# Combined blocks of the output weights made early and kept in DRAM; pair sums of y on VectorE

## The chip, the cores and the metric
The kernel runs on one core of one Trainium2 chip. The metric is device time in microseconds (us) of one execution. The kernel before took 882.3 us, the median of three runs (879.62 to 882.65).

Engines are named as in the profile: PE is TensorE (matmuls), PEld its weight loads, DVE is VectorE, ACT is ScalarE, POOL is GpSimd, and SP is the queue from which all DMAs here are issued.

## The reference
One layer on x, 2048 positions of 1024 channels, float32:

```python
h = rmsnorm(x, g_pre) * (1 + scale) + shift          # scale, shift, gate from c
gu, gv, gg, rq, rk, rv, rg = split(h @ w_in)         # seven parts of 512 columns
y_gmlp = gu * (tril(w_s) LN(gv) + b) * silu(gg)      # chunks of 128 positions, 4 groups
y_ret = GroupNorm(retention(rope(rq), rope(rk), rv)) * silu(rg)   # 4 heads, chunkwise
y = concat(y_gmlp, y_ret) @ w_out                    # 2048 x 1024 times 1024 x 1024
x = x + gate * rmsnorm(y, g_post)
```

The change touches the last product, y @ w_out, only.

## The kernel before, in words
**Precision.** Each float32 operand of a large product is split into a high part of reduced precision (`wh`, `yh`, `hh`, made by a copy on ACT) and a rest (`wl`, `yl`, `hl`, made by a subtraction on DVE). A product of two blocks is then three matmuls (`mm3`, L256 to L258), each with 512 columns.

**Halves and units.** The 2048 positions are worked in two halves. In each half four passes over h make retention's v, q and k and gMLP's v; then come six units of 28 ticks, which make the gates and u. A unit multiplies two by two blocks of weights with two by two blocks of h by a Strassen-Winograd scheme: seven products instead of eight, in the order of PRODUCTS, with sums of blocks on both sides (A11, S2, A12, S3, S1, A22, S4 on the one, B11, T2, B21, T3, T1, T4, B22 on the other), gathered in the PSUM banks X, Y and Z. A bank is reopened for a later product: the third product goes on in X, the fourth and sixth in Y, the seventh in Z. What is read from a bank in between (`s1` by a copy on ACT, `u2` and `u3` by adds on DVE, written `u` in the profile) must be read before the bank's next product starts. In the units POOL makes the sums of weight blocks (L241).

**The out stage.** y @ w_out uses the same scheme. Its A side are pairs of chunks: position block ch and position block ch + 4 of a half, eight pairs in all. The y blocks are spilled to DRAM (`yspill`, L614) and read back a pair at a time (`ya`, L624). `pair_sums` makes S1 to S4 of a pair (`ys`, L634): on DVE for the first group, which interleaves two pairs, and on POOL for the six single pairs behind it. Each of a pair's seven operands is then split (`yh` on ACT L643, `yl` on DVE L644), six ticks ahead of its product. `out_tail` reads the banks: adds (L694), squares with row sums on ACT (L691), the root on POOL (L698, L699), gains (L705), the result (L708) and its store (L710).

**Output weights.** 28 blocks (seven products times four of the inner dimension) of 128x512 are needed, and stay in SBUF once they are split. `pump` takes the next one in a fixed order: `wdma` loads it and the next two or three (L190), and `wsplit` splits it (L198, L201). B11, B21 and B22 are blocks of `wout`. The T blocks are combined by `osplit`: at T2 the blocks B12, B11 and B22 are loaded, and two DVE operations make T3 and T2 (L215, L216); T3 is kept in SBUF until its turn; T1 is made by one DVE operation at its own turn (L220), and T4 by one more from B21, loaded a second time (L224). The splits of a combined block start a tick later. B11 is pumped at the end of the fifth unit and the start of the sixth, T2, B21 and T3 in the sixth unit, T1, T4 and B22 in the first group, one block each second tick.

**What sets the order.** The instructions of PE, DVE, ACT and POOL stand in the order in which the program gives them, and each engine works through its own in order. The program goes by ticks: `slots.tick()` before each group of three matmuls runs what is due, and `slots.at(n, f)` makes f due n ticks later. A tick is three matmuls. SP's order is chosen by the compiler from what is ready; SP too works in order, so a DMA that waits holds those behind it.

**SBUF.** Most tiles of 128x512 come from one pool of 80 slots (`slot`).

Of the kernel before, what the change touches and what calls it, by code (L numbers as in the profile page):

```python
# [11 lines left out]
F32 = mybir.dt.float32  # L12
# [4 lines left out]
ALU = mybir.AluOpType  # L17
# [4 lines left out]
P = 128  # L22
# [23 lines left out]
PRODUCTS = (("B11", "A11"), ("T2", "S2"), ("B21", "A12"), ("T3", "S3"), ("T1", "S1"), ("T4", "A22"),  # L46
            ("B22", "S4"))
# [53 lines left out]
def tile_hybrid_layer(ctx: ExitStack, tc, x, xt, wm, wg, win, wun, wout, wst, cols, rows, pos, cst,  # L101
                      invf, out):
    nc = tc.nc
    V, S, G, T, SP = nc.vector, nc.scalar, nc.gpsimd, nc.tensor, nc.sync
# [4 lines left out]
    ps_m = ctx.enter_context(tc.tile_pool(name="ps_m", bufs=4, space=PSUM))  # L109
    ps_s = ctx.enter_context(tc.tile_pool(name="ps_s", bufs=4, space=PSUM))  # L110

    slots = Slots()
    ctx.enter_context(tc.manual_schedule(engines=ORDERED))

# [27 lines left out]
    def slot(name, shape=(512,), dtype=F32, pool=None):  # L142
        return (pool or big).tile([P, *shape], dtype, name=name, tag="s")
# [9 lines left out]
    def closed(n=1):  # L153
        for _ in range(n):
# [3 lines left out]
    raw, blocks = {}, {}  # L158
# [1 line left out]
    PER_HALF = IN_BLOCKS + len(UNITS) * len(PRODUCTS)  # L160
    OUT_BLOCKS = 2 * PER_HALF
    ALL_BLOCKS = OUT_BLOCKS + 4 * len(PRODUCTS)
    OUT_RAW = {"B11": ("B11",), "T2": ("B12", "B11", "B22"), "B21": ("B21",), "T3": (),
               "T1": (), "T4": ("B21",), "B22": ("B22",)}

    def place(i):
        if i >= OUT_BLOCKS:
            return "out", 0, i - OUT_BLOCKS
        half, i = divmod(i, PER_HALF)
        if i < IN_BLOCKS:  # L170
            return "in", half, i
        return "unit", half, i - IN_BLOCKS

    def wdma(i):
        kind, half, n = place(i)
        if kind == "unit":
            un = n // len(PRODUCTS)
            if (half, un) not in raw:
                raw[half, un] = {}
                for k, key in enumerate(("B11", "B12", "B22", "B21")):  # L180
                    t = raw[half, un][key] = slot("ur")
                    SP.dma_start(t, wun[un, (0, 1, 3, 2)[k]])
            return
        if i in raw or i in blocks:
            return
        if kind == "out":
            raw[i] = {}
            for key in OUT_RAW[PRODUCTS[n // 4][0]]:
                t = raw[i][key] = slot("or")
                SP.dma_start(t, wout[int(key[2]) - 1, 4 * int(key[1]) - 4 + n % 4])  # L190
            return
        raw[i] = slot("wr")
        SP.dma_start(raw[i], win[n // KB, n % KB])

    def split(i, r, eng, gap):
        hi, lo = slot("wh", dtype=F32R), slot("wl", dtype=F32R)
        blocks[i] = (hi, lo)
        S.copy(hi, r)  # L198

        def rest():  # L200
            eng.tensor_tensor(lo, r, hi.bitcast(F32), ALU.subtract)  # L201

        if gap:
            slots.at(gap - 1, rest)
        else:
            rest()

    kept = {}

    def osplit(i, n, eng, gap):  # L210
        r, (p, kb) = raw.pop(i), divmod(n, 4)
        what = PRODUCTS[p][0]
        if what == "T2":
            t3, t2, t1 = kept["T3", kb], kept["T2", kb], kept["T1", kb] = r["B12"], r["B11"], r["B22"]
            V.tensor_tensor(t3, t1, t3, ALU.subtract)  # L215
            V.tensor_tensor(t2, t3, t2, ALU.add)  # L216
            slots.at(1, lambda: split(i, t2, eng, gap))
        elif what == "T1":
            t = kept.pop((what, kb))
            V.tensor_tensor(t, t, kept["T2", kb], ALU.subtract)  # L220
            slots.at(1, lambda: split(i, t, eng, gap))
        elif what == "T4":
            t = r["B21"]
            V.tensor_tensor(t, t, kept.pop(("T2", kb)), ALU.subtract)  # L224
            slots.at(1, lambda: split(i, t, eng, gap))
        else:
            split(i, kept.pop((what, kb)) if what == "T3" else r[what], eng, gap)

    def wsplit(i, eng=V, gap=1):
        wdma(i)  # L230
        kind, half, n = place(i)
        if kind == "out":
            return osplit(i, n, eng, gap)
        if kind == "in":
            return split(i, raw.pop(i), eng, gap)
        r = raw[half, n // len(PRODUCTS)]
        what = PRODUCTS[n % len(PRODUCTS)][0]

        def combine(name, a, b):
            r[name] = slot("ut")  # L240
            G.tensor_tensor(r[name], r[a], r[b], ALU.subtract)  # L241

        if what == "T2":
            combine("T1", "B12", "B11")
            combine("T2", "B22", "T1")
        elif what == "T3":
            combine("T3", "B22", "B12")
        elif what == "T4":
            combine("T4", "B21", "T2")
        if what in ("T2", "T3", "T4"):  # L250
            slots.at(3, lambda: split(i, r[what], eng, gap))
        else:
            split(i, r[what], eng, gap)
# [9 lines left out]
    def pump(eng=V, gap=1, ahead=3):  # L263
        if done[0] < len(worder):
            wsplit(worder[done[0]], eng, gap)
            done[0] += 1
        for i in worder[done[0]:done[0] + ahead]:
            wdma(i)
# [334 lines left out]
            slots.at(delay + t, fn)  # L603


    ydram = ctx.enter_context(tc.tile_pool(name="ydram", bufs=1, space=bass.MemoryType.DRAM))
    yd = {}

    def yspill(half, part, cols):
# [7 lines left out]
    def pair_loads(half, ch):  # L617
        a = {}

        def load():  # L620
            for m in range(2):
                for part in range(2):
                    t = a[f"A{m + 1}{part + 1}"] = slot("ya", (4, P), pool=areas[0])
                    SP.dma_start(t, yd[half, part, m][:, ch, :, :])  # L624

        return a, load

    def pair_sums(a, ops, size, j):

        def op(out, x, y, how):  # L630
            def run():
                if out not in a:
                    a[out] = slot("ys", (4, P))
                (V if size > 1 else G).tensor_tensor(a[out], a[x], a[y], how)  # L634
                if out == "S3":
                    a.pop("A21")
            return run

        def part(key):
            def run():  # L640
                hi, lo = ops[key] = slot("yh", (4, P), F32R), slot("yl", (4, P), F32R)
                src = a[key]
                S.copy(hi, src)  # L643
                slots.at(0, lambda: V.tensor_tensor(lo, src, hi.bitcast(F32), ALU.subtract))  # L644
            return run

        def need(n):
            return 4 * (size * n + j)

        n = [need(i) for i in range(len(PRODUCTS))]  # L650
        return ((n[0] - 8, op("S1", "A21", "A22", ALU.add)), (n[0] - 6, part("A11")),
                (n[1] - 9, op("S2", "S1", "A11", ALU.subtract)), (n[1] - 6, part("S2")),
                (n[3] - 12, op("S3", "A11", "A21", ALU.subtract)), (n[2] - 6, part("A12")),
                (n[3] - 6, part("S3")), (n[6] - 17, op("S4", "A12", "S2", ALU.subtract)),
                (n[4] - 6, part("S1")), (n[5] - 6, part("A22")), (n[6] - 6, part("S4")))
# [456 lines left out]
    def prepare(group, at):  # L1112

        for j, (_, _, ops, a, load) in enumerate(group):
            slots.at(at - 20 + 4 * j, load)
            for t, fn in pair_sums(a, ops, len(group), j):
                slots.at(at + t, fn)
# [26 lines left out]
    for half in range(2):  # L1144
# [56 lines left out]
        for un in range(len(UNITS)):  # L1201
            if un == 0:
                for n, fn in enumerate(late):
                    slots.at(1 + 3 * (n // 2) + n % 2, fn)
            if un == 2:
                slots.at(5, partial(yspill, half, 0, range(HEADS)))
            if un == 4:
                slots.at(6, partial(yspill, half, 1, (0, 1)))
            if half == 0 and un in BUILD:
                for t, what, *args in BUILD[un]:  # L1210
                    slots.at(t, partial({"diag": diag1, "row": row1, "x": fetch1, "h": build1}[what],
                                        *args))
            if half == 1 and un == len(UNITS) - 1:
                groups = []
                for size in GROUPS_OUT:
                    groups.append([])
                    for i in range(size):
                        n = sum(GROUPS_OUT[:len(groups) - 1]) + i
                        groups[-1].append((*divmod(n, QUAD), {}, *pair_loads(*divmod(n, QUAD))))
                prepare(groups[0], len(PRODUCTS) * 4)  # L1220
            unit(half, un, up)
# [78 lines left out]
```

## Time and profile before

| | |
|---|---|
| three runs | 882.3, 882.65, 879.62 us |
| profiled execution, own time | 881.76 us |
| its span in the profile | 880.0 us |
| PE busy | 845.7 us (96%), 4074 instructions |
| DVE busy | 673.3 us (77%), 1275 instructions |
| ACT busy | 313.0 us (36%) |
| POOL busy | 358.1 us (41%) |
| granted TensorE clock, mean | 0.995 |
| DMA | 100.59 MB, mean 114 GB/s |

The profiled execution's own time is 1.76 us more than the span, which runs from the first to the last instruction in the profile. A busy share is a mean over stages with different limits. In the profile's rows `out<-in` gives the tiles that an instruction writes and reads, a name in brackets behind "idle before" is what ended a wait, and the line number is that of the kernel printed above. The second half's units run from 591 to 709 us, the out stage's first group from 709 to 752 us, and the six single pairs from there to 869 us.

### The profile page before, as it was taken

The page shows a single profiled execution, that of the slowest core. Times are in us where ns is not written, and L with a number is a line of the kernel's source. Part 1 is how long each engine was busy: PE and PEld are TensorE (multiplying, and loading weights), DVE is VectorE, ACT ScalarE, POOL GpSimd, SP SyncE. Part 2 cuts the span into 40 slices and gives each one's busy share as a digit, 9 for nine tenths or more (in the row PEclk, how much of TensorE's full clock was granted, in tenths as well). Part 3 has the DMA queues.
Part 4 walks back from the last instruction along what each step waited for, and adds up shares of the span by engine and source line. Part 5 has one row for each costly group of instructions (what it writes and reads, how often), then busy time and mean ns, then how long its engine had stood idle before and what let it go on. Part 6 is the DMA issues. An engine that isn't in the chain of part 4 may idle for free.

```text
span 880.0 us, 11841 instructions
## 1 busy us (share of the span) xinstructions
PE 845.7 (96%) x4074; PEld 696.3 (79%) x4074; DVE 673.3 (77%) x1275; ACT 313.0 (36%) x611; POOL 358.1 (41%) x403
## 2 busy tenths in 40 slices
PE   1999999999999999999999999999999999899996
PEld 0778888888888888888888888888888767688884
DVE  3989885665996768997786665897448898978885
ACT  4674223232363334431111221345343444333331
POOL 2031264345756236300443234675566000644551
PEclk9999999999999999999999999999999999999998
DMA  8971331310013424654222100011424854565422
GB/s 321 329 266 37 96 105 64 96 37 1 1 60 96 133 72 155 198 173 155 60 72 74 49 1 1 1 49 37 121 83 151 280 187 149 184 180 163 144 106 86
DMA packets 61884, 100.59 MB, mean 114 GB/s; under 512 B 5888, under 2 KB 22400, under 8 KB 61824
## 3 DMA queue, kind: packets, MB, share of 16 engines
q1 hardware_dynamic: 61824, 99.83, 34.6%
q8 instruction: 32, 0.52, 0.2%
q14 instruction: 28, 0.23, 0.1%
HBM read 83.03 MB, written 16.78 MB: 113 GB/s over the span
## 4 chain that ended last, share of the span: by engine, by line
PE 84%; DVE 6%; issue 3%; DMA 3%; ACT 2%; POOL 1%; SPq 0%; DVEq 0%; POOLq 0%; ACTq 0%
PE pqk L258 6%; PE pqk L256 6%; PE pqk L257 6%; PE pY L258 4%; PE pY L256 4%; PE pY L257 3%; PE pv L256 3%; PE pv L258 3%; PE pv L257 3%; PE prv L257 3%; PE prv L256 2%; PE pX L256 2%; PE prv L258 2%; PE pX L258 2%; PE pX L257 2%
## 5 line engine op out<-in xcount | busy, mean ns | idle before, releaser
L256 PE MATMUL pqk<-wh,hh 128*128 128x512 f32 x240 | 102.5, 427 | 0.0
L524 POOL TENSOR_TENSOR rA<-rA,rB 128x512 f32<-128x512 f32 x32 | 42.9, 1340 | 133.4 <-DVE rB L516 96.5
L258 PE MATMUL pqk<-wh,hl 128*128 128x512 f32 x240 | 94.7, 394 | 0.0
L257 PE MATMUL pqk<-wl,hh 128*128 128x512 f32 x240 | 93.8, 391 | 0.0
L538 ACT COPY qkT<-tp 128x512 f32<-128x512 f32 x32 | 18.8, 588 | 160.1 <-PE tp L529 160.1
L698 POOL TENSOR_SCALAR zrs<-zss 128x1 f32<-128x1 f32 x16 | 18.2, 1140 | 128.7 <-ACT jz L691 128.0
L201 DVE TENSOR_TENSOR wl<-wr,wh 128x512 fp32r<-128x512 f32 x62 | 63.0, 1030 | 0.2
L258 PEld LDWEIGHTS pqk<-wh,hl 128*128 128x128 f32 x240 | 45.0, 188 | 10.6
L256 PE MATMUL pv<-wh,hh 128*128 128x512 f32 x128 | 52.1, 407 | 0.0
L257 PEld LDWEIGHTS pqk<-wl,hh 128*128 128x128 f32 x240 | 45.5, 189 | 6.7 <-issue 0.2
L256 PEld LDWEIGHTS pqk<-wh,hh 128*128 128x128 f32 x240 | 45.4, 189 | 6.5 <-issue 0.2
L258 PE MATMUL pv<-wh,hl 128*128 128x512 f32 x128 | 50.1, 391 | 0.0
L257 PE MATMUL pv<-wl,hh 128*128 128x512 f32 x128 | 50.0, 390 | 0.0
L514 DVE TENSOR_TENSOR rA<-pqk,cos_t 128x512 f32<-128x512 f32 x28 | 19.3, 688 | 32.0 <-PE pqk L258 32.0
L201 DVE TENSOR_TENSOR wl<-ut,wh 128x512 fp32r<-128x512 f32 x48 | 42.9, 913 | 0.5 <-ACT wh L198 0.3
L582 DVE TENSOR_SCALAR yq<-o,gmv,grs 128x128 f32<-128x128 f32 x64 | 23.3, 405 | 23.9 <-POOL grs L575 23.9
L241 POOL TENSOR_TENSOR ut<-ur,ut 128x512 f32<-128x512 f32 x24 | 35.8, 1492 | 13.6 <-DVE yT L790 7.2
L461 ACT ACTIVATE vh<-pv,nbv,rsv 128x128 f32<-128x128 f32 x64 | 24.2, 457 | 47.4 <-POOL nbv L456 47.4
L256 PE MATMUL zY<-wh,yh 128*128 128x512 f32 x96 | 38.2, 398 | 2.2 <-DVE u L694 2.2
L198 ACT CAST wh<-ut 128x512 fp32r<-128x512 f32 x48 | 28.7, 621 | 31.7 <-POOL ut L241 31.7
L258 PE MATMUL zY<-wh,yl 128*128 128x512 f32 x96 | 38.3, 399 | 1.2 <-DVE yl L644 1.2
L790 POOL TENSOR_TENSOR yT<-yT,c 128x512 f32<-128x512 f32 x15 | 24.5, 1638 | 35.9 <-DVE c L810 25.8
(258 smaller groups left out, 2571.1 us busy)
## 6 DMA issues: line engine op xcount, KB each, us to landing
wr<-in_win SPq DMA_DIRECT2D x64, 256.0 KB, 3.9
ur<-in_wun SPq DMA_DIRECT2D x48, 256.0 KB, 3.5
slab<-in_wm SPq DMA_DIRECT2D x16, 512.0 KB, 6.2
ya<-yd SPq DMA_DIRECT2D x32, 256.0 KB, 3.8
xr<-in_x SPq DMA_DIRECT2D x16, 512.0 KB, 5.2
out<-xr SPq DMA_DIRECT2D x32, 256.0 KB, 2.8
or<-in_wout SPq DMA_DIRECT2D x28, 256.0 KB, 3.1
xt<-in_xt SPq DMA_DIRECT2D x24, 256.0 KB, 4.2
```

Of the source, the lines that this page charges most:

```text
L198: S.copy(hi, r)
L201: eng.tensor_tensor(lo, r, hi.bitcast(F32), ALU.subtract)
L241: G.tensor_tensor(r[name], r[a], r[b], ALU.subtract)
L256: T.matmul(ps, l[0], r[0], start=first, stop=False, skip_group_check=reopened)
L257: T.matmul(ps, l[0], r[1], start=False, stop=False, skip_group_check=reopened)
L258: T.matmul(ps, l[1], r[0], start=False, stop=last, skip_group_check=reopened)
L461: S.activation(vh[:, g, :], ps[:, g * P:(g + 1) * P], AF.Identity, bias=nb[:, g:g + 1], scale=rs[:, g:g + 1])
L514: V.tensor_tensor(A, ps.rearrange("p (g d) -> p g d", g=8), tab["cos"][:, ch, :].unsqueeze(1).broadcast_to([P, 8, 64]), ALU.mult)
L524: G.tensor_tensor(A, A, box["B"].rearrange("p g h d -> p (g h d)"), ALU.add)
L538: S.copy(qkT, box["tp"])
L582: V.tensor_scalar(yq[h][:, ch % QUAD, :], box["o"][:, i, :], mv[:, i, 0:1], rs[:, i:i + 1], ALU.subtract, ALU.mult)
L790: eng.tensor_tensor(y, y, by, ALU.mult)
```

## The change
The sums of the output weights' blocks are made in the second half's units 0 to 3, one kb each (`combined`): four raw blocks are loaded, four DVE operations make T3, T2, T1 and T4, each in place, and each is stored to a DRAM tile. In the last unit and the first group every block, T or raw, is then loaded from DRAM by one DMA and split like the blocks of the input weights; `osplit` and what it kept in SBUF are gone. `pair_sums` puts its sums on DVE for all groups. The DRAM pool is opened earlier in the program.

```diff
-            raw[i] = {}
-            for key in OUT_RAW[PRODUCTS[n // 4][0]]:
-                t = raw[i][key] = slot("or")
-                SP.dma_start(t, wout[int(key[2]) - 1, 4 * int(key[1]) - 4 + n % 4])
+            key, kb = PRODUCTS[n // 4][0], n % 4
+            raw[i] = slot("or")
+            SP.dma_start(raw[i], wsums[key, kb] if key[0] == "T" else wout_block(key, kb))
...
-    def osplit(i, n, eng, gap):
...
+    def combined(kb, at):
+
+        t = {}
+
+        def load():
+            for key in ("B12", "B22", "B11", "B21"):
+                t[key] = slot("tr")
+                SP.dma_start(t[key], wout_block(key, kb))
+
+        def op(out, a, b, how):
+            V.tensor_tensor(t[out], t[a], t[b], how)
+
+        def store(name, key):
+            wsums[name, kb] = ydram.tile([P, 512], F32, name=f"ws{name}{kb}")
+            SP.dma_start(wsums[name, kb], t[key])
+
+        slots.at(at, load)
+        for n, (name, *what) in enumerate((("T3", "B12", "B22", "B12", ALU.subtract),
+                                           ("T2", "B11", "B12", "B11", ALU.add),
+                                           ("T1", "B22", "B22", "B11", ALU.subtract),
+                                           ("T4", "B21", "B21", "B11", ALU.subtract))):
+            slots.at(at + 10 + 3 * n, partial(op, *what))
+            slots.at(at + 14 + 3 * n, partial(store, name, what[0]))
...
-        if kind == "out":
-            return osplit(i, n, eng, gap)
-        if kind == "in":
+        if kind != "unit":
             return split(i, raw.pop(i), eng, gap)
...
-                (V if size > 1 else G).tensor_tensor(a[out], a[x], a[y], how)
+                V.tensor_tensor(a[out], a[x], a[y], how)
...
+            if half == 1 and un < 4:
+                combined(un, 2)
```

## Rows read from the trace of the kernel before

**Rows 1.** The page, part 1: busy us (share of the span) and instructions.
```profile
PE 845.7 (96%) x4074; PEld 696.3 (79%) x4074; DVE 673.3 (77%) x1275; ACT 313.0 (36%) x611; POOL 358.1 (41%) x403
```

**Rows 2.** Stretches: length, then busy (instructions) of each engine, granted clock, DMA share, GB/s.
```profile
core 0: us, PE busy (x) PEld busy (x) DVE busy (x) ACT busy (x) POOL busy (x), PEclk, DMA share, GB/s
627.00:646.00 19.00, 19.00 (x85) 15.64 (x84) 7.95 (x12) 6.69 (x13) 10.68 (x8) 1.00 0.48 153
...
723.00:733.00 10.00, 8.27 (x35) 6.11 (x35) 9.69 (x17) 5.21 (x11) 0.00 (x0) 1.00 0.84 295
753.00:763.00 10.00, 8.00 (x33) 5.67 (x31) 9.87 (x12) 5.20 (x13) 8.54 (x7) 1.00 0.59 183
763.00:773.00 10.00, 9.28 (x34) 7.58 (x35) 6.84 (x10) 1.53 (x4) 1.27 (x1) 0.83 0.94 317
779.00:798.00 19.00, 19.00 (x85) 15.75 (x84) 15.59 (x21) 7.07 (x16) 9.76 (x9) 1.00 0.58 166
```

**Rows 3.** Instructions of PE in order of time: start us, us; first matmuls of products.
```profile
693.91 0.50 PE L256 MATMUL pX<-hh,wh 128*128 128x512 f32 x1
...
697.89 0.50 PE L256 MATMUL pY<-sh,wh 128*128 128x512 f32 x1 [0.94 <-DVE u L810]
...
708.90 0.39 PE L256 MATMUL zX<-wh,yh 128*128 128x512 f32 x1
...
735.78 0.39 PE L256 MATMUL zZ<-wh,yh 128*128 128x512 f32 x1
...
752.10 0.39 PE L256 MATMUL zX<-wh,yh 128*128 128x512 f32 x1
...
768.13 0.39 PE L256 MATMUL zZ<-wh,yh 128*128 128x512 f32 x1
...
776.29 0.39 PE L256 MATMUL zX<-wh,yh 128*128 128x512 f32 x1
...
795.33 0.39 PE L256 MATMUL zX<-wh,yh 128*128 128x512 f32 x1
```

**Rows 4.** PE's waits, 560 to 880 us: us in total, times, longest.
```profile
PE zX L258 <- DVE yl L644: 2.3, 4, 1.2
PE zY L256 <- DVE u L694: 2.2, 1, 2.2
```

**Rows 5.** Instructions on tile `or`: count, duration ns min/median/max, first and last start.
```profile
L190 SPq DMA_DIRECT2D or<-in_wout x28: 327/382/579, 673.4 to 728.5; - x28
...
L224 DVE TENSOR_TENSOR or<-or x4: 684/691/694, 719.6 to 725.6; 128x512 f32<-128x512 f32 x4
...
DMA to landing us min/median/max: 2.5/3.1/6.7
```

**Rows 6.** DMA issues, 700 to 740 us: count, KB each, median us to landing.
```profile
or<-in_wout SPq DMA_DIRECT2D x8, 256.0 KB, 5.4
```

**Rows 7.** Waits, 700 to 735 us: us in total, times, longest.
```profile
ACT wh L198 <- DMA or<-in_wout: 4.2, 5, 1.6
```

**Rows 8.** Instructions of DVE in order of time, 745 to 770 us.
```profile
748.63 1.16 DVE L705 TENSOR_TENSOR c<-c,gg 128x512 f32<-128x512 f32 x1 [0.79 <-ACT jz L691]
749.71 1.78 DVE L644 TENSOR_TENSOR yl<-ya,yh 128x512 fp32r<-128x512 f32 x1
...
758.26 0.68 DVE L644 TENSOR_TENSOR yl<-ya,yh 128x512 fp32r<-128x512 f32 x1
...
761.22 1.75 DVE L644 TENSOR_TENSOR yl<-ys,yh 128x512 fp32r<-128x512 f32 x1
762.89 0.68 DVE L694 TENSOR_TENSOR u<-zY,s 128x512 f32<-128x512 f32 x1
```

**Rows 9.** Unit 0 of the second half in order of time: DVE, then PE.
```profile
604.97 0.68 DVE L810 TENSOR_TENSOR u<-pY,s 128x512 f32<-128x512 f32 x1
...
606.30 0.39 PE L256 MATMUL pY<-hh,wh 128*128 128x512 f32 x1
```

**Rows 10.** Instructions on tile `ya`: count, duration ns min/median/max, starts.
```profile
L634 POOL TENSOR_TENSOR ys<-ya x12: 1286/1298/1715, 748.0 to 853.4; 128x512 f32<-128x512 f32 x12
```

**Rows 11.** Groups of DVE's instructions, 779 to 855 us: busy, mean ns, idle before.
```profile
L705 DVE TENSOR_TENSOR c<-c,gg 128x512 f32<-128x512 f32 x13 | 11.2, 864 | 10.5 <-ACT jz L691 10.5
```

More of the change, by code (lines that the diff above doesn't have):

```diff
@@ L110, in tile_hybrid_layer @@
     ps_s = ctx.enter_context(tc.tile_pool(name="ps_s", bufs=4, space=PSUM))
+    ydram = ctx.enter_context(tc.tile_pool(name="ydram", bufs=1, space=bass.MemoryType.DRAM))
     slots = Slots()
@@ L162, in tile_hybrid_layer, with wout_block @@
     ALL_BLOCKS = OUT_BLOCKS + 4 * len(PRODUCTS)
-    OUT_RAW = {"B11": ("B11",), "T2": ("B12", "B11", "B22"), "B21": ("B21",), "T3": (),
-               "T1": (), "T4": ("B21",), "B22": ("B22",)}
+    wsums = {}
+    def wout_block(key, kb):
+        return wout[int(key[2]) - 1, 4 * int(key[1]) - 4 + kb]
     def place(i):
@@ L206, in split @@
             rest()
-    kept = {}
-    def osplit(i, n, eng, gap):
[L211 to L227, printed above, removed]
+    def combined(kb, at):
[16 more added lines that the diff above has]
+            slots.at(at + 14 + 3 * n, partial(store, name, what[0]))
     def wsplit(i, eng=V, gap=1):
@@ L603, in ret_pair @@
             slots.at(delay + t, fn)
-    ydram = ctx.enter_context(tc.tile_pool(name="ydram", bufs=1, space=bass.MemoryType.DRAM))
     yd = {}
```

## The prediction, made before the result was known

> **What bounds the kernel now.** I began with the page's busy shares: PE is busy for 845.7 of 880.0 us [rows 1], so only its idle time can be won, and the question is where that lies. The stretches say it. From 627 to 646 us, a unit of the second half, PE is busy throughout while DVE works 7.95 of 19 us; from 723 to 733 us, in the out stage's first group, DVE works 9.69 of 10 us and PE only 8.27; from 753 to 763 us it is 9.87 against 8.00, with POOL at 8.54; from 779 to 798 us PE is full again, DVE at 15.59 of 19 [rows 2]. Then I took the starts of products on PE. In the steady pairs two pairs' starts lie 19.04 us apart [rows 3]: 84 matmuls, 2.72 us for a product's twelve. Against that pace three places are late:
> - the third product of the last unit takes 3.98 us, 1.26 too long;
> - the first four products of the two-pair group take 26.88 us instead of 21.76, 5.12 too long;
> - the first four of the next pair take 16.03 instead of 10.88, 5.15 too long. Part of this is the clock: in 763 to 773 us the granted clock is 0.83 of its upper level, 2.4 GHz, a stretch at 1.2 GHz behind PE's longest wait [rows 2, 4].
>
> Together 11.5 us, the most that can be won here. Who is waited for: DVE each time, `u` and `yl` [rows 4]. DVE is the bound in these 80 us, PE everywhere else around them.
>
> **The change, part by part.** Durations are of the profiled execution, whose own time is 881.76 us; the three runs' median is 882.3 us, so 0.5 us lies between the bases.
>
> *Sixteen DVE operations leave the crowd.* T2 and T3 (eight operations) were made in the last unit, T1 and T4 (eight more, L220 and L224) in the first group, 0.69 us each [rows 5]. Back to back they overlap a little: 17 operations in 9.69 us are one each 0.57 us [rows 2]; I take 0.60, so 4.8 us leave the last unit and 4.8 us the first group.
>
> Last unit: `u` waits behind T2's subtractions and behind splits that wait for them. With these gone it follows its product: 1.26 us come back; bounds 0 and 1.26.
>
> First group: DVE alone would give back all of the 5.12 us, since 4.8 us of its own work and the backlog carried in go. What is late next is ACT. Until now T3 and T1 were kept in SBUF; now every block comes from DRAM straight into ACT's `wh` copy. A load goes out two blocks ahead, one block each second tick: four ticks, 12 matmuls, 2.72 us. In the nearest rows such a load takes 3.1 us over the kernel [rows 5] and 5.4 us in this stretch [rows 6]. So ACT stands still for up to 2.7 us at a block, and it already waits 4.2 us for these loads [rows 7]. Queued behind on ACT are the `yh` copies, issued six ticks (4.1 us) before PE needs them; take off a copy and a DVE subtraction, 0.69 us each by L224's size [rows 5], and 2.7 us are left, less one or two queued DVE operations, so the hold exceeds the slack by 0.6 to 1.2 us. I count 0.9 us at two places, once among T1 and T4 and once at the last raw blocks: 1.8 us remain and 3.3 come back. Bounds: 5.1 (loads land in time) and 0 (ACT's holds replace every DVE wait).
>
> The Trainium skill's page "DMA: Bandwidth & Descriptors", section "Anatomy of one DMA — SWDGE (gpsimd) path", gives a DMA some 2.0 us fixed and its bytes at 436 GB/s; an estimate from it for 256 KB is 2.6 us, which would just land within the lead, and the sum below would be 1.8 us lower. The trace disagrees where it matters: 5.4 us here [rows 6]; the page's fit is for POOL's path, and these go through SP.
>
> *The same sixteen operations come into units 0 to 3 of the second half.* There DVE is free for more than half the time in units 1 to 3 ([rows 2], 627 to 646 us); four operations a unit, 2.8 us, or 7 us if each is caught by a POOL operation as `yl` is at 749.71 us (1.78 against 0.68 us [rows 8]), fit in its 11 idle us. Cost nothing; cover gone only if a unit's `u` came over 2 us late. Unit 0 is different: its DVE still works off the sums. There the add `u` starts at 604.97 us and ends at 605.65, and PE reopens that bank at 606.30 [rows 9]: 0.65 us of slack. T3's and T2's operations (ticks 12 and 15) stand ahead of that add (tick 16) and shift it by 1.2 us: 0.6 us of PE wait. Bounds: 0 (a gap I don't see) and 3 us (a raw block lands late and holds DVE).
>
> *DMA.* 16 loads and 16 stores of 256 KB more in units 0 to 3, at SP's 0.38 us an issue [rows 5] 12 us of a queue over 76 us; the DMA engines are at 0.48 there [rows 2]. A store waits for its DVE operation, issued four ticks before; behind it on SP are the spills and the next unit's `ur` loads, for which POOL's combining waits. Even one of DVE's long operations is over in 1.78 us [rows 8], less than those four ticks (2.7 us), and a unit's blocks are made a unit ahead: 0, and 1.8 us as the upper bound. In the out stage 28 loads stay 28: T2 takes four instead of twelve, T3 and T1 four each that were none, T4 four as before. PE never waits for the stores; a load of a T block finds its store long done.
>
> *Pair sums on DVE.* Six pairs' four sums each, 24 operations, cost POOL 1.3 to 1.7 us apiece and will cost DVE what a sum of this shape costs it, 0.69 [rows 5, 10]. Per steady pair DVE gains 2.4 us of work at its back-to-back pace. It loses what POOL now takes from it: the same `yl` takes 1.78 or 1.75 us beside POOL's sums and 0.68 without [rows 8]; four such cases per pair are some 3 us. So steady pairs stay at PE's pace: nothing (no gain is to be had where PE is full; the upper bound is rival 2).
>
> The boundary pair: from 748.6 us to `u` at 762.89, 16 DVE operations run without a gap, five of them long (first, second and last in [rows 8]: 1.16, 1.78, 1.75 us; 8.17 us for the five, where short ones take 3.55), 4.6 us too much. That goes, four sums come (2.4 us): `u` comes 2.2 us earlier, about what PE waited for it [rows 4]; but PE, without its earlier small waits, comes 0.9 us earlier too. I leave 1.0 us of wait and expect the clock not to fall, as it didn't after the shorter waits (0.94 us at 697.89 [rows 3], with the clock whole until 763 us). 4.15 of 5.15 us come back; bounds 0 and 5.15.
>
> **The sum.** 1.26 + 3.3 + 4.15 − 0.6 = 8.1 us; 881.76 − 8.1 = 873.6 us.
>
> **Rivals.**
> 1. *ACT waits where DVE waited.* T blocks come late, ACT's holds replace DVE's backlog in the first group, and a wait there is again long enough for the clock to fall. For it: loads take 5.4 us with a lead of 2.7, and the spills of the last y blocks stand in the same queue. Against it: the T2 burst of twelve loads is gone. The first group gives nothing, the boundary half (2.1 us), unit 0 costs 0.6: 881.76 − 1.26 − 2.1 + 0.6 = 879.0 us, no change.
> 2. *DVE becomes the bound of the six single pairs: slower.* If the operations that are long today stay long without POOL's sums, a steady pair has 15.59 us of DVE work [rows 2] plus 4 × 0.69, and the gain `c` still waits 10.5 us over 13 for ACT's squares [rows 11], 0.8 us each and three a pair: 15.59 + 2.8 + 2.4 = 20.8 us against 19.04. Six pairs lose 1.75 us each, 10.5 us, and the boundary gives nothing: 881.76 + 10.5 − 1.26 − 3.3 + 0.6 = 888.3 us. It decides once a pair's DVE work and waits pass 19.04 us, that is when less than 1.75 us of the stretching goes. Against it: with POOL at 0.00 DVE does 17 operations in 9.69 us, in the steady pairs 21 in 15.59 us with POOL at 9.76 [rows 2].
> 3. *The long DVE operations are gone, and ACT and the loads hide behind them too*: everything comes back but unit 0, 881.76 − 11.5 + 0.6 = 870.8 us.
>
> **Chances.** My forecast 0.5, rival 3 0.18, rival 1 0.22, rival 2 0.10. About 0.5% (4.4 us) is what this kernel's measurement tells from no change. Faster by more: 0.68 (forecast and rival 3); within 0.5%: 0.22; slower: 0.10. The range runs from 870.5 (all comes back) to 881.5 us (rival 1 with unit 0 at its upper bound); it leaves rival 2 out.
>
> **What would show it.** Right: `u` of the last unit follows its product and L201 no longer waits for L215 or L224; in the first group PE near 9.5 of each 10 us; `yl` and `xr` at 0.68 to 0.75 us everywhere from 750 us on; the granted clock 1.00 around the boundary; POOL with nothing but `zrs` in the out stage; steady pairs still 19.04 us apart. Wrong: steady starts over 19.1 us apart (rival 2); ACT's waits for `or` loads well over 8 us with PE waiting for `yl` behind them (rival 1); PE waits for `u` of over 1 us in unit 0 or for `ur` in units 1 to 4.

## The result, and the profile after

The changed kernel takes 874.43 us (median of 4 runs, 873.88 to 875.26) against 882.17 us (4 runs, 879.62 to 882.65) of the kernel before: ratio 0.9919, 95% interval 0.9898 to 0.994, so 7.7 us faster. The forecast was 873.6 us. The profiled execution took 874.51 us (before: 881.76), and its span 872.7 us (before: 880.0). The kernel's lines stand three or four further down now (split L201/L204, pair sums L637, `yh`/`yl` L646/L647, adds of a group L697, gain L708, result L711, adds of a unit L813), and the blocks made early are loaded at L218, combined at L221 and stored at L225.

The page's part 1 after, then stretches of the trace after (length, busy us and instructions of each engine, granted clock, DMA share, GB/s); they answer to [rows 1, 2]:

```profile
PE 843.7 (97%) x4074; PEld 696.6 (80%) x4074; DVE 673.1 (77%) x1299; ACT 311.1 (36%) x611; POOL 329.8 (38%) x379
```

```profile
716.00:726.00 10.00, 9.14 (x39) 6.94 (x38) 7.17 (x12) 5.78 (x11) 0.00 (x0) 1.00 0.98 358
746.00:756.00 10.00, 9.62 (x43) 7.62 (x41) 9.74 (x17) 4.07 (x10) 6.23 (x6) 1.00 0.47 148
763.00:773.00 10.00, 10.00 (x46) 8.29 (x45) 6.84 (x11) 4.39 (x11) 3.26 (x3) 1.00 0.62 214
766.00:785.00 19.00, 19.00 (x86) 15.72 (x85) 15.10 (x25) 6.95 (x16) 4.39 (x4) 1.00 0.63 201
```

DVE is as busy as before in total (673.1 against 673.3 us), although it runs 24 instructions more. POOL lost 28.3 us. Where DVE was full and PE starved, PE now has 9.14 and 9.62 of 10 us, the clock is whole behind the boundary, and in a steady pair DVE does 25 operations in 15.10 us where it did 21 in 15.59 [rows 2].

All of PE's waits after, 560 to 880 us (us in total, times, longest), beside [rows 4]:

```profile
PE zX L260 <- ACT yh L646: 0.8, 1, 0.8
PE pY L260 <- DVE u L813: 0.5, 1, 0.5
PE zY L260 <- DVE u L697: 0.5, 1, 0.5
PE zX L260 <- ACT s L727: 0.4, 1, 0.4
```

First matmuls of products after (start, duration), beside [rows 3]:

```profile
719.58 0.39 PE L260 MATMUL zX<-wh,yh 128*128 128x512 f32 x1
...
726.46 0.39 PE L260 MATMUL zY<-wh,yh 128*128 128x512 f32 x1
...
751.24 0.39 PE L260 MATMUL zY<-wh,yh 128*128 128x512 f32 x1
...
754.50 0.50 PE L260 MATMUL zX<-wh,yh 128*128 128x512 f32 x1 [0.38 <-ACT s L727]
...
758.06 0.47 PE L260 MATMUL zY<-wh,yh 128*128 128x512 f32 x1 [0.54 <-DVE u L697]
...
774.47 0.39 PE L260 MATMUL zX<-wh,yh 128*128 128x512 f32 x1
...
793.51 0.39 PE L260 MATMUL zX<-wh,yh 128*128 128x512 f32 x1
```

The way to read them is the same as in the prediction: 2.72 us for a product of one pair, 5.44 us for one of two. From 719.58 to 726.46 is 6.88 us, 1.44 too long. From 751.24 to 754.50 is 3.26, 0.54 too long, and from there to 758.06 is 3.56, 0.84 too long. From 774.47 to 793.51 is 19.04 us: a steady pair costs what it cost. Done for every product from 600 us on, with places under 0.12 us left out, this gives what PE lost against its own pace:

| us that PE lost | before | after | forecast |
|---|---|---|---|
| units 0 and 1 of the second half | 0 | 0.88 + 0.36 | 0.6 |
| unit 4 | 0 | 0.27 | 0 |
| last unit | 1.39 | 0 | 0.13 |
| first group of two pairs | 5.12 | 1.74 | 1.8 |
| boundary pair | 5.15 | 1.38 | 1.0 |
| sum | 11.7 | 4.6 | 3.5 |

The 7.0 us that fell away between these rows (11.66 less 4.63) are nearly the whole effect: the span fell by 7.3 us, the profiled executions' own times by 7.25. The rest stands ahead of the table: the product behind which it starts opens at 596.88 us instead of 597.24.

### The profile page after: what moved, and what is told of

Read it like the earlier page. It is cut to its first block, busy times and chain, and to the rows that moved or that the text cites. A ratio compares the mean times of both kernels' runs of the same rounds, so it can differ in the third digit from the quotient of the medians.

```text
span 872.7 us, 11879 instructions
## 1 busy us (share of the span) xinstructions
PE 843.7 (97%) x4074; PEld 696.6 (80%) x4074; DVE 673.1 (77%) x1299; ACT 311.1 (36%) x611; POOL 329.8 (38%) x379
## 4 chain that ended last, share of the span: by engine, by line
PE 84%; DVE 6%; DMA 3%; issue 3%; ACT 2%; POOL 1%; SPq 0%; DVEq 0%; POOLq 0%; ACTq 0%
PE pqk L262 6%; PE pqk L260 6%; PE pqk L261 6%; PE pv L260 3%; PE pv L262 3%; PE pY L260 3%; PE pv L261 3%; PE pY L262 3%; PE pY L261 3%; PE prv L261 3%; PE prv L260 3%; PE prv L262 3%; PE pX L261 2%; PE pX L262 2%; PE pX L260 2%
## 5 line engine op out<-in xcount | busy, mean ns | idle before, releaser
L701 POOL TENSOR_SCALAR zrs<-zss 128x1 f32<-128x1 f32 x16 | 20.0, 1248 | 151.4 <-ACT jz L694 151.4
L204 DVE TENSOR_TENSOR wl<-wr,wh 128x512 fp32r<-128x512 f32 x62 | 62.9, 1028 | 0.2
L262 PEld LDWEIGHTS pqk<-wh,hl 128*128 128x128 f32 x240 | 45.0, 188 | 10.6
L204 DVE TENSOR_TENSOR wl<-ut,wh 128x512 fp32r<-128x512 f32 x48 | 42.6, 906 | 2.5 <-ACT wh L201 2.2
L201 ACT CAST wh<-ut 128x512 fp32r<-128x512 f32 x48 | 28.7, 620 | 36.6 <-POOL ut L245 36.5
L245 POOL TENSOR_TENSOR ut<-ur 128x512 f32<-128x512 f32 x24 | 34.6, 1443 | 12.9 <-DMA ur<-in_wun 9.9
L694 ACT ACTIVATE jz<-c 128x512 bf16<-128x512 f32 x24 | 15.1, 631 | 67.9 <-DVE c L697 67.9
```

Source lines behind the costliest of these rows:

```text
L262: T.matmul(ps, l[1], r[0], start=False, stop=last, skip_group_check=reopened)
L701: G.tensor_scalar(r, ss[:, m, 0:1], ss[:, m, 1:2], EPS, ALU.add, ALU.add)
```

## The experiments

The theory: DVE was the bound in three places; the early blocks free it in the last unit and in the first group, the sums on DVE free it at the boundary, because POOL's reading had stretched DVE's own operations. Rival: the gain is one thing, a DVE freed of either burden, and one edit alone brings nearly all of it. Losses named below are found as in the table, from each run's own trace.

**The sums alone.** The kernel before, with one line changed:

```diff
-                (V if size > 1 else G).tensor_tensor(a[out], a[x], a[y], how)
+                V.tensor_tensor(a[out], a[x], a[y], how)
```

> The kernel before with the pair sums of all groups on DVE; the T blocks are made in the last unit and first group as before. My theory: the boundary pair lost 5.15 us because POOL's sums stretched DVE's operations; that alone goes, so its first four products lose about 1.4 us as in the changed kernel, while the last unit's 1.26 and the first group's 5.1 us stay: 882.2 - 3.8 = 878.4 us, with yl and xr at 0.68 to 0.75 us from 750 us on and steady pairs still 19.04 us apart. Rival: the boundary's backlog came from the T blocks' DVE work in the first group, so the boundary stays at about 5 us and the time at 882 us. Rival of the prediction (DVE the bound of the single pairs): steady pairs over 19.1 us apart, 888 us.

Measured: 878.6 us (877.73 to 879.74, 7 runs) against 881.85 (14 runs), ratio 0.9962, interval 0.9951 to 0.9973. One stretch at the boundary, then a group of DVE's instructions from 779 to 855 us (busy us, mean ns, idle before):

```profile
753.00:763.00 10.00, 9.06 (x39) 6.88 (x38) 9.87 (x17) 4.58 (x11) 4.08 (x4) 1.00 0.76 245
```

```profile
L644 DVE TENSOR_TENSOR yl<-ys,yh 128x512 fp32r<-128x512 f32 x16 | 10.9, 683 | 0.0
```

The row has the same 9.87 us of DVE as [rows 2] for that stretch, but 17 instructions in it instead of 12: a full engine says nothing until its operations are counted. The last unit (1.39 us lost) and the first group (4.97) stay as before; the boundary falls from 5.15 to 1.44.

**The blocks alone.** The changed kernel with the sums of single pairs back on POOL:

```diff
-                V.tensor_tensor(a[out], a[x], a[y], how)
+                (V if size > 1 else G).tensor_tensor(a[out], a[x], a[y], how)
```

> The changed kernel with the pair sums of single pairs back on POOL. My theory: the last unit loses nothing and the first group some 1.7 us as in the changed kernel, unit 0 and 1 lose their 1.2 us, and the boundary loses about 5 us as before: 882.2 - 1.3 - 3.4 + 1.2 = 878.7 us, so that the gains of this run and of the sums alone add up to the whole (about 3.5 and 3.8 of 7.7 us). Rival (the boundary's loss was the T blocks' backlog): the boundary gains too, and this run alone comes to 875 us.

Measured: 878.04 us (876.57 to 879.03, 8 runs), ratio 0.996, interval 0.9946 to 0.9974. The last unit loses nothing, the first group 1.98, units 0 and 1 0.86 + 0.34, unit 4 0.61. At the boundary PE waits for the same add as before, and as long, but loses 3.4 us and not 5.15. PE's wait, then a stretch behind it:

```profile
PE zY L260 <- DVE u L697: 2.2, 1, 2.2
```

```profile
765.00:767.00 2.00, 2.00 (x11) 1.65 (x10) 1.07 (x2) 0.03 (x1) 0.00 (x0) 1.00 0.82 167
```

The gains add as far as the medians can tell: 3.3 and 3.8 us make 7.1, against 7.7 for both at once; the 3.8 is rough, since the eight times of this kernel lie in two groups (below). The places say it more firmly: the sums alone change the boundary and leave the last unit and the first group as they were; the blocks alone clear the last unit and most of the first group and leave the boundary's wait as it was. Two causes, then, each at its own place; the rival falls. One thing was not as expected: the clock stayed whole behind this wait, which is why the boundary lost less.

**Not in unit 0.** The sixteen operations start one unit later:

```diff
-            if half == 1 and un < 4:
+            if half == 1 and un in (1, 2, 3):
                 combined(un, 2)
+                if un == 1:
+                    combined(0, 14)
```

> The changed kernel with no block sums in unit 0: unit 1 makes two kb, 12 ticks apart, units 2 and 3 one each. My theory: unit 0's loss of 0.7 to 0.9 us is the two DVE operations ahead of the add that reopens Y; it goes, and with units 1 to 3 having idle DVE time nothing comes in its place: 873.5 us, the add of unit 0 at about 604.6 us again. Rival: a late raw block or SP order made that loss, or unit 1 (which lost 0.36 us in the changed kernel by a wait for POOL) loses as much more with eight operations: 874.4 us or above.

Measured: 873.49 us (873.22 to 873.9, 4 runs), ratio 0.9907, interval 0.9891 to 0.9923. Unit 0's and unit 1's losses (1.24 us) are gone: `u` starts at 604.70 instead of 605.83. But unit 4, which loses 0.27 us in the changed kernel, loses 1.18 (1.05 of it in one product). So the 873.5 us that I expected, with nothing in place of the 1.24, came out by luck: the first group and the boundary happen to lose about 0.3 us less in this trace, and the profiled executions differ by 0.61 us where the medians differ by 0.94. PE's wait in unit 4, then a DVE row ahead of it and the same row of the changed kernel:

```profile
PE pY L260 <- DVE u L813: 0.9, 1, 0.9
```

```profile
665.75 1.77 DVE L204 TENSOR_TENSOR wl<-ur,wh 128x512 fp32r<-128x512 f32 x1
```

```profile
666.73 0.68 DVE L204 TENSOR_TENSOR wl<-ur,wh 128x512 fp32r<-128x512 f32 x1
```

So the sums were the cause in unit 0. Unit 4's loss does not come from unit 1's double load, as far as the rows go. Up to the add `c` ahead of this `wl` DVE is 0.97 us ahead of the changed kernel (664.55 against 665.52), as PE is. The `wl` then runs beside POOL's `yT` (665.30 to 666.98) and takes 1.77 us, and the next add is only 0.07 us ahead (667.45 against 667.52). The `u` for which PE waits starts at 677.65 (changed kernel: 677.54), and PE, 0.96 us earlier than there, stands still for it. What PE wins in front, DVE loses again where its operations meet POOL's. How they meet moves with little: with the blocks alone, whose units are those of the changed kernel, unit 4 lost 0.61.

**A longer lead for the loads.** Loads of `or` go out earlier, six blocks ahead instead of three in the last unit and instead of two in the out stage:

```diff
-                    pump()
+                    pump(ahead=6 if (half, un) == (1, 5) else 3)
...
-                        pump(V, 1, 2)
+                        pump(V, 1, 6)
```

> The changed kernel with the blocks of the output weights loaded six ahead instead of three (last unit) and two (first group). My theory: the first group's remaining 1.7 us are ACT held by loads that go out 2.7 us ahead and behind spills; with six ahead ACT's waits for these loads fall from 13.8 us to under 4 and the first group loses under 0.5 us: 873.0 us. Rival: the DMA engines are full there (share 0.98 from 716 to 726 us), so loads issued earlier only queue longer (landing over 7 us instead of 5.5) and ACT's waits and the 1.7 us stay: 874.4 us.

Measured: 872.49 us (872.29 to 872.6, 4 runs), ratio 0.9895, interval 0.9879 to 0.9911. The first group loses nothing. Its stretch, then ACT's waits for `or` from 690 to 735 us, first with the longer lead and then in the changed kernel:

```profile
716.00:726.00 10.00, 10.00 (x46) 8.29 (x45) 10.00 (x18) 7.05 (x16) 0.00 (x0) 1.00 1.02 393
```

```profile
ACT wh L201 <- DMA or<-wsT: 6.2, 2, 3.1
...
ACT wh L201 <- DMA or<-in_wout: 0.2, 1, 0.2
```

```profile
ACT wh L201 <- DMA or<-wsT: 8.5, 6, 2.8
ACT wh L201 <- DMA or<-in_wout: 5.3, 5, 1.8
```

What PE lost in this group was the loads' lateness: eleven holds of ACT become three, and PE is full. ACT's waits fell to 6.4 us and not under 4, but the two long ones that are left lie in the last unit (they end at 701 and 706 us), where PE loses nothing. All this comes although the loads themselves hardly land faster: from 690 to 735 us a stored block takes 5.9 us in the median and one from the weights 4.5, against 5.6 and 5.4 us in the changed kernel.

**POOL's adds beside DVE's.** DVE keeps the sums, and POOL does the like of them again beside the single pairs' sums, two tiles read, into a slot that nobody reads:

```diff
                 V.tensor_tensor(a[out], a[x], a[y], how)
+                if size == 1:
+                    dm = slot("dm", (4, P))
+                    G.tensor_tensor(dm, a["A11"], a["A12"], how)
```

> The changed kernel, and beside each of the 24 sums that DVE now makes for the single pairs POOL makes one of the same shape into a tile that nobody reads. My theory (POOL's two-input operations on SBUF stretch DVE's; that was the boundary's loss and would have been the rival's slower kernel): DVE's yl and xr are long again (1.7 us instead of 0.7), a steady pair needs 14.8 + 2.4 us of DVE work and waits, 2.4 for the sums and some 3 of stretching already counted in it, so over 19.04 us: pairs 19.5 to 20.8 us apart and the boundary at 5 us or more, 880 to 888 us. Rival (the gain came from taking the sums out of POOL's queue, where they stood behind the roots): nothing on PE waits for these operations, so 874.4 us and steady pairs 19.04 us apart.

Measured: 890.1 us (889.31 to 890.9, 4 runs) against 880.48 (7 runs), ratio 1.0105, interval 1.0083 to 1.0126. Rows of DVE in a pair, then a row of POOL there (three adds from 781.23 to 786.03 us):

```profile
781.43 1.77 DVE L637 TENSOR_TENSOR ys<-ya,ys 128x512 f32<-128x512 f32 x1
783.13 1.77 DVE L650 TENSOR_TENSOR yl<-ys,yh 128x512 fp32r<-128x512 f32 x1
784.82 0.68 DVE L700 TENSOR_TENSOR u<-zY,s 128x512 f32<-128x512 f32 x1
```

```profile
781.23 4.80 POOL L640 TENSOR_TENSOR dm<-ya 128x512 f32<-128x512 f32 x3
```

Beside POOL's add a DVE operation with both inputs in SBUF takes 1.77 us; `u`, one of whose inputs lies in PSUM, keeps its 0.68 us though POOL is still adding. It takes no tile that both read: POOL reads `ya`, and the stretched `yl` reads `ys` and `yh`. PE's wait, and the same product of two pairs in a row:

```profile
PE zY L260 <- DVE u L700: 10.5, 6, 3.8
```

```profile
781.30 0.39 PE L260 MATMUL zX<-wh,yh 128*128 128x512 f32 x1
...
802.07 0.39 PE L260 MATMUL zX<-wh,yh 128*128 128x512 f32 x1
```

A pair now takes 20.77 us, and the next three starts lie 20.86 to 20.89 apart. That is rival 2 come true, at the price that it was given (20.8 us): the changed kernel escapes it because POOL stopped reading, not because DVE had room. That the price fits so closely is partly luck: it was 18.4 us of DVE work and 2.4 of waiting, and from 781.30 to 802.07 us DVE works for 17.68 and is idle for 3.09. The boundary loses 8.6 us here, more than the 5.15 that the rival had left there.

**POOL's writes.** The same place, but POOL only sets the slot to a constant, once or three times:

```diff
-                    G.tensor_tensor(dm, a["A11"], a["A12"], how)
+                    G.memset(dm, 0.0)
```

> As the run before, with a memset of the same 128x512 on POOL in place of the operation that reads two tiles. If what stretches DVE is that POOL reads SBUF, DVE's operations stay at 0.7 us and the time at 874.4 us; if any long POOL operation does it (or POOL's queue: the roots stand behind the memsets as well), it is as slow as the run before, 880 us or more.

> As the changed kernel, but beside each of the single pairs' sums POOL writes a constant into a spare 128x512 slot three times (no input read, nobody reads the slot): 24 places, 72 writes of some 0.52 us each, about 1.57 us of POOL per sum, as much as one of its two-input adds (1.54 us). Theory, what stretches DVE's operations is POOL reading two tiles from SBUF and not POOL being busy or writing: yl stays at 0.68 to 0.70 us, xr at 0.75, the steady pairs at 19.04 us, time 874.5 us, within 1 us of the changed kernel. Rival, any work of POOL on tiles of this size for about 1.5 us per sum does it, and the single writes were only too short: steady pairs over 20 us apart, yl near 0.97 us, 885 to 890 us.

Measured: 874.71 us with one (874.43 to 875.51, 4 runs; before 880.48, ratio 0.9932, interval 0.9908 to 0.9955) and 875.37 us with three (875.02 to 876.16, 4 runs; before 881.79, ratio 0.9932, interval 0.9916 to 0.9947). The first of POOL's three lines of writes (durations in ns min/median/max; the other two have 527 in the median), and two of DVE's groups beside the three writes, from 779 to 850 us (busy us, mean ns, idle before):

```profile
L640 POOL MEMSET dm<- x24: 519/523/529, 744.5 to 850.5; 128x512 f32 x24
...
```

```profile
L652 DVE TENSOR_TENSOR yl<-ys,yh 128x512 fp32r<-128x512 f32 x14 | 9.6, 682 | 0.0
...
L716 DVE SCALAR_TENSOR_TENSOR xr<-c,zrs,xr 128x512 f32<-128x512 f32 x10 | 7.2, 746 | 0.0
```

The single write left a gap in the argument: 0.52 us are less than an add's 1.54. Three of them fill 1.57 us at each sum, and DVE's operations still take 0.68 and 0.75 us. POOL being busy is not what stretches them.

**One tile read.** POOL multiplies one tile by one:

```diff
-                    G.tensor_tensor(dm, a["A11"], a["A12"], how)
+                    G.tensor_scalar(dm, a["A11"], 1.0, 1.0, ALU.mult, ALU.mult)
```

> As the changed kernel, but beside each of the single pairs' sums POOL multiplies one 128x512 tile by one into a spare slot (one input read, nobody reads the slot), 24 more operations. If a single read from SBUF by POOL is enough to hold DVE, yl comes out over 0.8 us in the mean, the steady pairs lie over 19.3 us apart and the time is 880 to 890 us, in proportion to how long POOL's operation takes (the two-input add took 1.54 us and cost 15.4 us in all). If only a two-input operation does it: yl at 0.68 to 0.70 us, 19.04 us, 874.5 us within 1 us. I lean to the first: DVE's subtraction has two inputs of its own, and one reader more may be all it takes.

Measured: 876.07 us (875.68 to 877.02, 4 runs) against 881.79, ratio 0.9941, interval 0.9922 to 0.9959. The size that I leaned to was wrong, the mechanism not. Rows of DVE, then POOL's row beside them (two multiplications):

```profile
794.34 1.10 DVE L637 TENSOR_TENSOR ys<-ya,ys 128x512 f32<-128x512 f32 x1
795.37 1.09 DVE L650 TENSOR_TENSOR yl<-ys,yh 128x512 fp32r<-128x512 f32 x1
```

```profile
794.16 1.75 POOL L640 TENSOR_SCALAR dm<-ya 128x512 f32<-128x512 f32 x2
```

Reading one tile does stretch DVE's operations, but this one lasts 0.65 us in the median, and beside it `ys` and `yl` come out 0.41 us longer instead of 1.09. That much the pairs nearly absorb: of four intervals between steady pairs two are 19.35 and 19.40 us and two stay at 19.04.

**Two orders inside the pairs.** A single pair's S4 sum ten ticks before its product instead of 17, and the results of the first pair four ticks later:

```diff
-                (n[3] - 6, part("S3")), (n[6] - 17, op("S4", "A12", "S2", ALU.subtract)),
+                (n[3] - 6, part("S3")), (n[6] - (17 if size > 1 else 10), op("S4", "A12", "S2", ALU.subtract)),
...
+        early = (half, ch) == (0, 0)
...
-                                                 (10, lambda: result(0, 0, tmp["g11"])),
-                                                 (11, lambda: result(0, 1, tmp["c12"]))))
+                                                 (10 + 4 * early, lambda: result(0, 0, tmp["g11"])),
+                                                 (11 + 4 * early, lambda: result(0, 1, tmp["c12"]))))
```

> The changed kernel with only the order at the boundary changed: S4 of a single pair seven ticks later, the first group's first result (two DVE operations) four ticks later, so that three DVE operations of 0.6 to 0.66 us stand behind the add u that PE waits for instead of ahead of it. My theory: the boundary's remaining 1.4 us are DVE's queue ahead of that add; it comes 1.9 us earlier, PE loses at most 0.4 us there: 873.4 us. Rival: the add waits for its PE product or ACT's copy instead, and the 1.4 us stay.

Measured: 873.66 us (873.3 to 874.3, 4 runs) against 880.48, ratio 0.9919, interval 0.9899 to 0.9938. PE's wait for `u` at the boundary is gone, and the boundary loses 0.69 us instead of 1.38 (0.4 was expected); what is left there is the wait for ACT's copy `s`. In time that is too little for these runs: the ratio is that of the changed kernel. The trace shows it, the time does not.

**All of it together.** The longer lead, those two orders, and the early blocks in units 1 and 2 only, two rounds each:

```diff
-            if half == 1 and un < 4:
-                combined(un, 2)
+            if half == 1 and un in (1, 2):
+                combined(2 * un - 2, 2)
+                combined(2 * un - 1, 14)
```

> Loads six ahead, block sums in units 1 and 2 alone (two kb each, 12 ticks apart), S4 of a single pair seven ticks later and the first group's first result four ticks later. My theory: the parts are separate, so unit 0's and 1's 1.2 us, the first group's 1.7 and about 1 of the boundary's 1.4 us go: 874.4 - 3.9 = 870.5 us, PE full from unit 0 to the last pair but for some 0.5 us. Rival: units 1 and 2 can't take eight DVE operations each beside POOL's (or unit 4 loses 1 us as when unit 0 was left out), 871.5 us or above.

Measured: 871.04 us (870.55 to 871.16, 4 runs) against 880.48, ratio 0.9887, interval 0.9868 to 0.9906. It is 9.4 us faster than the kernel before. The changed kernel itself was not run beside it; the run with the two orders, which differs from it in nothing else, took 873.66 us beside it. The longer lead alone (ratio 0.9895) can't be told from it by the intervals. PE's only wait from 560 us on:

```profile
PE pY L260 <- DVE u L814: 0.2, 1, 0.2
```

Its losses are 0.36 us in units 2 and 3, 0.50 in unit 4 and 0.41 at the boundary, 1.3 in all.

## Why the prediction was right

**The last unit.** Forecast: 1.26 us back. All of it came, 0.13 more with it. DVE's row of the add:

```profile
695.30 0.69 DVE L813 TENSOR_TENSOR u<-pY,s 128x512 f32<-128x512 f32 x1 [0.26 <-PE pY L262]
```

DVE now waits for the product instead of the product's bank for DVE; the add ends at 695.99, and PE opens that bank again at 697.82 without a wait.

**The first group.** Forecast: 3.3 of 5.12 us back, since ACT's holds for late loads take DVE's place; 1.8 remain. Measured: 3.38 back, 1.74 remain, by that mechanism, as the longer lead shows. That the sum fits to 0.06 us is luck: in the seven other traces with the same lead and the early blocks this group loses 1.24 to 2.00 us. The chain, ACT's rows:

```profile
720.10 0.62 ACT L201 CAST wh<-or 128x512 fp32r<-128x512 f32 x1 [1.79 <-DMA or<-wsT]
722.06 0.62 ACT L201 CAST wh<-or 128x512 fp32r<-128x512 f32 x1 [1.33 <-DMA or<-wsT]
722.58 0.61 ACT L646 CAST yh<-ya 128x512 fp32r<-128x512 f32 x1
```

Two holds in a row push the `yh` copy to 722.58; it ends at 723.19, and PE's `zX` goes on at 723.25. Where it sat was half right: I counted 0.9 us once among the T blocks and once at the last raw blocks; nearly all of it came at the T blocks. ACT's waits for loads of `or` grew to 13.8 us, well past the 8 us that I named as the sign of rival 1, and yet PE lost 1.7: most of the eleven holds lay within the slack of the copies behind them. What I overlooked is that ACT's copies of these blocks had waited as long before, only for someone else: from 690 to 735 us 10.6 us for DVE's operations that made the T blocks (3.7 L216, 3.1 L220, 3.8 L224) and 4.2 for loads, 14.8 in all. A sum of an engine's waits was the wrong sign to name; what counted is how far holds in a row push the one copy that PE needs next.

**The boundary.** Forecast: 4.15 of 5.15 us back, and no fall of the clock; measured 3.77, and the clock whole. Of these 3.77 us, 1.69 are the product that ran at the lower clock in the profiled execution of before; behind the same wait the kernel with the blocks alone kept its clock, so this part of the gain belongs to that execution and not surely to the sums. The reason given, that POOL's sums stretch DVE's operations, was read from five long operations and is now shown by the runs with POOL's adds, writes and reads. The Trainium skill's page "SBUF — State Buffer", section "Who interferes with whom", has the rule: a DVE instruction with two SBUF inputs contends with a GpSimd instruction that reads SBUF, not with one that only writes it. All of it agrees with the runs: 1.77 us beside adds, 1.10 beside the shorter read, 0.68 beside writes, and 0.68 for `u` with one input in SBUF. Counted from the pair's first product, `u` starts 8.71 us behind it instead of 10.79, 2.1 us earlier (forecast: 2.2); PE waits 0.54 us for it and loses 0.84 (forecast: 1.0). What I left out are the 0.54 us lost at ACT's copy `s`. Of these, 0.38 were lost there before as well; with the sums alone it is 0.60, with the blocks alone 0.34, with the longer lead 0.28, and what sets it is not shown.

**Unit 0, and the unit behind it.** Forecast: 0.6 us of wait at the add `u`. Its rows after, which answer to [rows 9], DVE and then PE:

```profile
602.39 0.68 DVE L221 TENSOR_TENSOR tr<-tr 128x512 f32<-128x512 f32 x1
...
605.23 0.68 DVE L221 TENSOR_TENSOR tr<-tr 128x512 f32<-128x512 f32 x1
605.83 0.68 DVE L813 TENSOR_TENSOR u<-pY,s 128x512 f32<-128x512 f32 x1
```

```profile
606.66 0.47 PE L260 MATMUL pY<-hh,wh 128*128 128x512 f32 x1 [0.55 <-DVE u L813]
```

The two operations stand where they were put, and PE waits 0.55 us. Against its own pace it loses 0.71 us at this stop and 0.17 in the product behind it, 0.88 in all. What I had not followed is the unit's next add, `c`. A third block sum (T1's, the first row below) stands ahead of it, so it starts at 608.24 us where it had started at 606.77, and a chain of four engines hangs on it:

```profile
607.63 0.68 DVE L221 TENSOR_TENSOR tr<-tr 128x512 f32<-128x512 f32 x1
608.24 0.68 DVE L813 TENSOR_TENSOR c<-pZ,u 128x512 f32<-128x512 f32 x1
...
608.95 0.63 ACT L801 ACTIVATE c<-c 128x512 f32<-128x512 f32 x1 [7.00 <-DVE c L813]
...
609.66 1.61 POOL L793 TENSOR_TENSOR yR<-yR,c 128x512 f32<-128x512 f32 x1 [7.74 <-ACT c L801]
...
611.24 1.28 POOL L245 TENSOR_TENSOR ut<-ur 128x512 f32<-128x512 f32 x1
612.60 1.29 POOL L245 TENSOR_TENSOR ut<-ur,ut 128x512 f32<-128x512 f32 x1
...
613.92 0.62 ACT L201 CAST wh<-ut 128x512 fp32r<-128x512 f32 x1 [2.48 <-POOL ut L245]
...
614.58 1.11 DVE L204 TENSOR_TENSOR wl<-ut,wh 128x512 fp32r<-128x512 f32 x1 [1.34 <-ACT wh L201]
```

POOL's `yR` stands ahead of the next unit's combining in POOL's order, so a late add makes a late `wl` (614.58 us, where it had been 612.85), and unit 1 loses 0.36 us at 615.74. With the sums out of unit 0 POOL's combining starts at 609.22 instead of 611.24, and unit 1 loses nothing. That the units behind unit 0 cost nothing was the step that failed, by 0.6 us with unit 4's 0.27, whose cause I did not follow up.

**Steady pairs and the rivals.** 19.04 us, as forecast, with `yl` at 0.683 and `xr` at 0.744 us in the mean. Rival 2's mechanism and price were right and its condition did not hold. Rival 1 was real in its first half (the holds) and did not reach its price; rival 3 lacked the loads' lateness, and with it removed, and the rest in order, the last version comes to a ratio of 0.9887, which is 871.8 on the prediction's base of 881.76, near the 870.8 us of rival 3. By the table the misses are 0.3 us in unit 0, 0.6 in the units behind it and 0.4 at the boundary, less 0.2 in the last unit and the first group: 1.1 us, of which 0.9 show between 873.6 and the profiled 874.51.

## What to carry to other kernels

Before an engine's busy share is taken as its bound, count its operations and compare the same operation in two stretches: 12 and 17 operations both filled 9.87 us, and moving work onto the "full" engine made it faster, since the engine that had done that work was what slowed it. When a load replaces a value that was kept in place, compare the load's landing time in that stretch with its lead, and then with the slack of what is queued behind the first instruction that uses it. When operations are put ahead of an add, follow the add's result through every engine's order to the next stage, not only to the next reader.

## What the runs showed beside this

The clock is not settled by the length of one wait. Before, PE waited 2.2 us for `u` [rows 4] and the granted clock fell. The stretch of the kernel before that has its floor:

```profile
765.00:767.00 2.00, 2.00 (x6) 1.55 (x5) 2.00 (x4) 0.00 (x0) 0.00 (x0) 0.50 1.01 398
```

That is 1.2 GHz instead of 2.4: 6 matmuls in 2 us. With the blocks alone PE waited as long, in the same place, and kept 1.00, with 11 matmuls in 2 us. The product at the lower clock lost 1.69 of the 5.15 us of the profiled execution of before. The kernel with the blocks alone ran in 876.57 to 877.32 us four times and in 878.77 to 879.03 four times, nothing between; that the clock makes this gap of some 2 us is argued, not shown, as only one of those executions has a trace. The mean granted clock, which is known for each, fits but overlaps: 0.996 to 0.998 in the faster four, 0.995 to 0.996 in the slower.

Loads of 256 KB that land in 3.1 us in the median over the kernel [rows 5] took 4.5 to 5.9 us from 690 to 735 us, where the DMA engines were at 0.98 to 1.02 and moved 358 to 393 GB/s in the busiest stretch. Sending them out earlier helped all the same: with six blocks of lead they landed no sooner, and PE lost nothing in the first group.
